# Two product tiles in turn, half a contraction apart, and activations moved by 64 bytes

## The chip, the cores and the metric

The kernel runs on one core of a Trainium2 chip. The metric is device time in microseconds (us) of one execution, lower is better. Engines are named as in the profile: PE is TensorE (matmuls), PEld its weight loads, DVE is VectorE, ACT is ScalarE, POOL is GpSimd, SP issues most DMAs.

## What is computed

A decoder trunk of two residual layers over 256 tokens of width 2048, all in float32. Layer 0 is "even" (an RG-LRU group and an RWKV-7 group behind one input projection), layer 1 is "odd" (an mLSTM block). Each is followed by a gated convolutional FFN. The change works in the odd layer, and by its second part in every product that reads the normed activations:

```
def mlstm_layer(x, norm, w_in, conv_w, conv_b, w_q, w_k, w_v, w_if, b_if, ln_w, skip, w_out):
    h = rms_norm(x, norm)                                  # (256, 2048)
    xm, z = jnp.split(h @ w_in, [C_WIDTH], axis=-1)        # w_in: 2048 x 8192, C_WIDTH 4096
    xc = jax.nn.silu(causal_dwconv(xm, conv_w, conv_b))
    ... # q, k, v, gates, the chunkwise mLSTM per head, layer norm, skip: hs
    return x + (hs * jax.nn.silu(z)) @ w_out               # w_out: 4096 x 2048

def conv_ffn(x, norm, w_gate, w_up, conv_w, conv_b, w_down):
    h = rms_norm(x, norm)
    u = jax.nn.silu(causal_dwconv(h @ w_gate, conv_w, conv_b)) * (h @ w_up)
    return x + u @ w_down
```

## The kernel before

**Tiles.** Everything is held transposed: 128 features on the partitions, 256 tokens along the free dimension. A weight matrix is cut into blocks of 128 x 128, 16 of them to a chunk of 128 x 2048 floats (1024 KB). `chunk` loads one from SP's queue into a `raw` tile (2 buffers) and splits it into a high part `wh` and a low part `wl` of the float32r type, in 4 pieces of 512 columns: ACT rounds (L243), DVE subtracts (L244). `wh` and `wl` have 2 buffers each, so a chunk's parts can be made when the chunk before the last is used up. An activation tile is split likewise: `x[k]`, `ux[k]` and `yx[k]` are tiles of 128 x 2 x 256, and the low part stands ahead of the high part.

**A block step.** One block of weights times one activation tile costs two matmuls in the wide form: `wh` times both parts (512 columns moved, into both halves of a PSUM bank) and `wl` times the high part (256 columns). Each matmul loads its 128 x 128 weights first. The products come in two orders:

- `mm3` (L247 to L261) does one output tile after another; within it each k runs low (L255), then high (L257), only the first k high (L254), then low. `project` (the odd layer's input product `oin`, 64 tiles of 16 blocks, in two stages: 32 tiles `xm`, then 32 tiles `z`) and `flat` (the odd layer's output product `oout`, 16 tiles of 32 blocks, and the even layer's two output products `eoa`, `eob`) use it. The even layer's input product `ein` uses the narrow form of `mm3`: three matmuls of 256 columns (L259 to L261).
- `mm3_pair` (L305 to L313) does two output tiles at once: high, high (L311), low, low (L313), both with the same `x[k]`. The FFN uses it: `fgu` (gate and up, moved operand `x`) and `fd` (down, moved operand `ux`), in tiles named `mp`.

**What sets the order.** The code emits instructions in program order, and the tile framework schedules them onto the engines; each engine then runs its own list in order. Side work is written as generators; `tick` lets each of them emit one more step, once in 4 block steps (`TICK`). In the odd layer's first stage the side work is `head_tile` (per tile: a convolution on ACT and DVE, L406 and L409, and the small products `pv` L932, `pr` L941, `sc` L947); in the second it is `heads_out` (the attention of one head after the other). A finished tile is read out of PSUM by `scaled` (ACT copy L424, DVE add L425, DVE multiply by the norm L427) or by `add_residual` (two DVE adds, L432). The pool `mm_ps` has 3 PSUM banks, tile name `mm`.

**Where the operands lie.** The pools `const`, `raw`, `parts` and `act` are opened in this order and stand behind one another in SBUF; the pools of the layers come behind `act`. `act` holds the residual, `x0` to `x15`, a few work tiles, and, by way of `rstd_steps` and `rsqrt`, the tiles `ms` and `rsq` of 2 floats a partition, each in a slot of 32 bytes. In the built program `wh` and `wl` begin 64 bytes past a multiple of 128, and so do all `x[k]`; `ux`, the odd layer's `yx` and 7 of `eob`'s 8 `yx` begin at a multiple of 128.

Of the kernel before, what the change touches and what calls it, by code (L numbers as in the profile page):

```python
# [17 lines left out]
F32 = mybir.dt.float32  # L18
# [6 lines left out]
P = 128  # L25
T = 256
D = 2048
KD = D // P
# [3 lines left out]
CW = 4096  # L32
# [7 lines left out]
CHEADS = 8  # L40
CTILES = 4
TICK = 4
# [4 lines left out]
SW = [4, 2]  # L47
OWAITS = [5, 2, 4]
AWAITS = [0, 4, 0, 1, 1, 3]


def wait(n):
    for _ in range(n):
        yield
# [52 lines left out]
class Builder:  # L107
    def __init__(self, tc, io, ctx):
        self.tc, self.nc, self.io = tc, tc.nc, io
        self.tile_pool = lambda **k: tc.tile_pool(reuse_waits="tile", **k)  # L110
        nc = self.nc
        self.n = 0
        pool = lambda name, bufs, **k: ctx.enter_context(self.tile_pool(name=name, bufs=bufs, **k))
        self.const = pool("const", 1)
        self.raw = pool("raw", 2)
        self.parts = pool("parts", 2)
        self.act = pool("act", 1)
        self.mm_ps = pool("mm_ps", 3, space=PSUM)
        self.vec_sb = self.const.tile([P, NV], F32, name="vec_sb")
        self.cons = {}  # L120
        self.load_con("con", self.const)
        self.x = [None] * KD
        self.sumsq = None
        self.rstd = None
        self.tasks = []
        self.norm_psum = lambda: self.psum_mm()[:, 0]
# [176 lines left out]
                self.tick()  # L303


    def mm3_pair(self, ps, w, c, x, start, stop):
        TE = self.nc.tensor
        hi = [w[0][:, i:i + P] for i in c]
        lo = [w[1][:, i:i + P] for i in c]
        for i in range(2):  # L310
            TE.matmul(ps[:, i], hi[i], x, start=start, stop=False)  # L311
        for i in range(2):
            TE.matmul(ps[:, i, 1], lo[i], x[:, 1], start=False, stop=stop)  # L313
# [51 lines left out]
    def rstd_steps(self):  # L365
        nc, a = self.nc, self.act
        yield from wait(SW[0])
        ps = self.norm_psum()
        for i in range(2):
            nc.tensor.matmul(ps[:, i:i + 1], self.sumsq[:, i * P:i * P + P], self.con("ones")[:, 0:1],  # L370
                             start=True, stop=True)
        ms = a.tile([P, 2], F32, name=self.name("ms"), tag="ms")
        nc.vector.tensor_scalar(ms, ps[:, 0:2], 1.0 / D, EPS, op0=ALU.mult, op1=ALU.add)
        r = self.rsqrt(a, ms, 2)
        yield from wait(SW[1])
        self.rstd = self.row_bcast(self.norm_psum, a, r, "rstd")

# [482 lines left out]
    def odd(self, gain, folded, fold_pool):  # L860
        nc, tc = self.nc, self.tc
        V, A, TE = nc.vector, nc.scalar, nc.tensor
        io = self.io
        with ExitStack() as es:
            big = es.enter_context(self.tile_pool(name="odd", bufs=1))
            big_tile = lambda dt, n: big.tile([P, CTILES, T], dt, name=self.name(n), tag="big", bufs=17)
            self.load_con("con_odd", big)
            raws, xcs, vs = [], [], []
            gates = big.tile([P, 2, 16], F32, name="gates")
            with ExitStack() as e1:  # L870
                sml = e1.enter_context(self.tile_pool(name="odd1", bufs=2))
                psr = e1.enter_context(self.tile_pool(name="odd1_ps", bufs=2, space=PSUM))
                psa = e1.enter_context(self.tile_pool(name="odd1_acc", bufs=1, space=PSUM))
                wl, wv, fa, fv = folded
                bdm = self.con("bdmask").rearrange("p (g j) -> p g j", j=4)
                four = lambda w: w.unsqueeze(1).to_broadcast([P, 32, 4])
                nc.gpsimd.memset(gates, 0.0)
                ops = (four, bdm, wl, wv, fa, fv)
                self.norm_psum = lambda: psr.tile([P, T], F32, name=self.name("np"), tag="pr")
                ps = self.projections(io["oin"], CHEADS * CTILES)  # L880
                for h in range(CHEADS):
                    xc4, v4 = big_tile(F32, "xc"), big_tile(F32, "v")
                    vt = v4.rearrange("p a b -> p (a b)").rearrange("p (s c) -> p s c", s=2)
                    raw = big.tile([P, 384], F32, name=self.name("raw"), tag="sc", bufs=CHEADS)
                    st = {}
                    for q in range(CTILES):
                        xm = self.scaled(sml, next(ps), 3, "xm", 3)
                        last = self.start(self.head_tile(h, q, xm, xc4[:, q], vt, raw, gates, st, ops, sml, psr, psa))
                    raws.append(raw)
                    xcs.append(xc4)  # L890
                    vs.append(vt)
                self.finish(last)
            fold_pool.close()
            yx = []
            with ExitStack() as e2:
                sml = e2.enter_context(self.tile_pool(name="odd2", bufs=2))
                one = e2.enter_context(self.tile_pool(name="odd2c", bufs=1))
                psw = e2.enter_context(self.tile_pool(name="odd2_ps", bufs=3, space=PSUM))
                pss = e2.enter_context(self.tile_pool(name="odd2_ps2", bufs=2, space=PSUM))
                pw = lambda *s: psw.tile(list(s), F32, name=self.name("pz"), tag="pz")  # L900
                pst = lambda *s: pss.tile(list(s), F32, name=self.name("pt"), tag="pt")
                zs = {}
                nums = self.start(self.heads_out(one, sml, pw, pst, gates, raws, vs, xcs, zs, big_tile, yx))
                for ct in range(CHEADS * CTILES):
                    while len(zs) >= 6:
                        self.tick()
                    z = self.scaled(sml, self.project(io["oin"][32 + ct]), 0, "z", 6)
                    A.activation(z, z, AF.Silu)
                    zs[ct] = z
                self.finish(nums)  # L910
                self.flat(io["oout"], 32, KD, yx, lambda m, ps: self.add_residual(m, ps, gain))

    def head_tile(self, h, q, xm, xc, vt, raw, gates, st, ops, sml, psr, psa):

# [144 lines left out]
    def attend(self, h, sml, pw, pst, raw, v, crow, gm):  # L1059
# [5 lines left out]
        TE.matmul(ps, self.con("ones")[0:8], ch, start=True, stop=True)  # L1065
        yield from wait(AWAITS[0])
        d = sml.tile([P, 384], F32, name=self.name("dec"), tag="dec")
# [4 lines left out]
        V.scalar_tensor_tensor(out=d, in0=raw, scalar=512.0 ** -0.5, in1=d, op0=ALU.mult, op1=ALU.mult)  # L1072
        yield from wait(AWAITS[1])
        ones = self.con("ones")[:, 0:1]
        st = sml.tile([P, 2, 2], F32, name=self.name("st"), tag="st")
        for s in range(2):
# [4 lines left out]
            V.tensor_copy(out=st[:, 0, s:s + 1], in_=ps)  # L1081
        yield from wait(AWAITS[2])
        num = sml.tile([P, CTILES, T], F32, name=self.name("num"), tag="num", bufs=1)
        acc = None
        for q in range(CTILES):
# [8 lines left out]
            else:  # L1094
                V.tensor_tensor(out=sq, in0=acc, in1=sq, op=ALU.add)
                acc = sq
            yield from wait(AWAITS[3])
        yield from wait(AWAITS[4])
        for s in range(2):
# [10 lines left out]
        rs = self.rsqrt(sml, var, 2)  # L1110
        yield from wait(AWAITS[5])
        return self.row_bcast(lambda: pst(P, T), sml, rs, "sbc"), num
# [31 lines left out]
def _by_cols(w):  # L1144

    k, m = w.shape
    return np.ascontiguousarray(w.reshape(k // P, P, m // P, P).transpose(2, 1, 0, 3)).reshape(m // P, P, -1)


def _flat(w):  # L1150

    k, m = w.shape
    t = w.reshape(k // P, P, m // P, P).transpose(2, 0, 1, 3).reshape(-1, 16, P, P)
    return np.ascontiguousarray(t.transpose(0, 2, 1, 3)).reshape(-1, P, 2048)


def _pairs(ws):

    n, k, _, _ = ws.shape
    t = ws.reshape(n, k // P, P, 2, P).transpose(0, 1, 3, 2, 4).reshape(-1, 16, P, P)  # L1160
    return np.ascontiguousarray(t.transpose(0, 2, 1, 3)).reshape(-1, P, 2048)
# [8 lines left out]
def _arrange(I):  # L1170
    I = {k: np.asarray(v) for k, v in I.items()}
    z = lambda *s: np.zeros(s, np.float32)
    o = {"xT": np.ascontiguousarray(I["x"][0].T.reshape(KD, P, T).transpose(1, 0, 2)), **_constants()}
    w = I["even_w_in"][0]
# [4 lines left out]
    m = I["b_mu"][0]  # L1179
# [6 lines left out]
        pieces += [w[:, cols(j)], w[:, AW + j * P:AW + j * P + P]]  # L1186
    o["ein"] = _by_cols(np.concatenate(pieces, 1))
    o["eoa"], o["eob"] = _flat(I["even_w_out"][0][:AW]), _flat(I["even_w_out"][0][AW:])
    o["oin"], o["oout"] = _by_cols(I["odd_w_in"][0]), _flat(I["odd_w_out"][0])
    for l in range(2):  # L1190
        by = lambda n: I[n][l].reshape(D, NF, P).transpose(1, 0, 2)
        o[f"fgu{l}"] = _pairs(np.stack([by("ffn_w_gate"), by("ffn_w_up")], 2))
# [44 lines left out]
```

## Time and profile before

| | |
|---|---|
| median of 3 runs | 2620.32 us (2619.95 to 2620.73) |
| profiled execution, its time / its span | 2621.55 us / 2619.7 us |
| busy in the span | PE 99%, PEld 87%, DVE 71%, ACT 56%, POOL 5% |
| granted TensorE clock | 0.997 of full speed |
| even layer (`ein`, `eoa`, `eob` and side work) | up to 500 us |
| first FFN: `fgu`, `fd` | 500 to 991, 991 to 1234 us |
| odd layer: `xm`, `z`, `oout` | 1234 to 1465, 1465 to 1686, 1687 to 1868 us |
| second FFN: `fgu`, `fd` | 1868 to 2360, 2360 to 2603 us |

The span is the time from the first to the last instruction of the profiled execution. PE's busy share says that it seldom waits for another engine, not that its matmuls follow one another as closely as they could: a record's length holds the pipeline too, and the next matmul starts before it ends. So a product's pace is read here from the starts of its matmuls.

### The profile page before, as it was taken

The numbers are of one execution on the slowest core, as the hardware profiler recorded it, in microseconds if no ns is written. First come the engines' busy times: TensorE is split into PE (matmuls) and PEld (weight loads), VectorE is DVE, ScalarE is ACT, GpSimd is POOL, SyncE is SP. The second block draws the span as 40 slices with busy tenths as digits, with TensorE's granted clock in tenths as the row PEclk, the third lists the DMA queues.
The fourth block names the chain that finished last, engine by engine and source line by source line (L and its number), as shares of the span: only waits on it lengthen the run. The fifth ranks groups of instructions, "written<-read, shape, count | busy, mean of one in ns | idle before, by whom it ended". The sixth has DMA issues, their size and how long they took to land.

```text
span 2619.7 us, 43129 instructions
## 1 busy us (share of the span) xinstructions
PE 2587.5 (99%) x16438; PEld 2272.8 (87%) x16438; DVE 1859.0 (71%) x4205; ACT 1459.0 (56%) x3071; POOL 137.9 (5%) x402
## 2 busy tenths in 40 slices
PE   9999999999999999999999999999999999999997
PEld 8888887888888888888888888888888888888886
DVE  7988888888667665555777787855667666775554
ACT  6766673655555554444666766644455555554443
POOL 1122111000000000000000000000000000000000
PEclk9999999999999999999999999999999999999999
DMA  6434434565555555555444344455555555555553
GB/s 209 154 108 129 134 105 141 185 217 205 185 189 193 193 193 190 189 185 197 149 144 153 134 148 160 144 203 184 181 189 193 193 193 185 187 189 195 184 199 132
DMA packets 67696, 454.41 MB, mean 173 GB/s; under 512 B 9328, under 2 KB 10352, under 8 KB 14240
## 3 DMA queue, kind: packets, MB, share of 16 engines
q1 hardware_dynamic: 62064, 441.69, 48.5%
q0 software_dynamic: 4416, 7.85, 1.1%
q8 instruction: 129, 2.11, 0.3%
q10 hardware_dynamic: 1008, 2.11, 0.2%
q14 instruction: 79, 0.65, 0.1%
HBM read 448.70 MB, written 2.10 MB: 172 GB/s over the span
## 4 chain that ended last, share of the span: by engine, by line
PE 82%; issue 11%; DVE 4%; ACT 1%; POOL 1%; DMA 0%; DVEq 0%; POOLq 0%; ACTq 0%
PE mp L311 31%; PE mp L313 15%; PE mm L257 14%; PE mm L255 8%; PE mm L259 2%; PE mm L260 2%; PE mm L261 2%; PE mm L254 1%; PE sc L947 1%; DVE wl L244 1%; PE pw L669 1%; PE pv L932 1%; PE pz L1087 1%; PE pr L941 1%; POOL rsq L381 0%
## 5 line engine op out<-in xcount | busy, mean ns | idle before, releaser
L244 DVE TENSOR_TENSOR wl<-raw,wh 128x512 fp32r<-128x512 f32 (+1 forms) x1680 | 1091.7, 682 | 511.3 <-ACT wh L243 509.8
L243 ACT CAST wh<-raw 128x512 fp32r<-128x512 f32 (+1 forms) x1680 | 952.7, 617 | 693.4 <-PE mp L311 540.5
L311 PE MATMUL mp<-x,wh 128*128 128x512 f32 x2816 | 884.7, 395 | 0.0
L313 PEld LDWEIGHTS mp<-x,wl 128*128 128x128 f32 x2816 | 529.0, 188 | 125.0
L313 PE MATMUL mp<-x,wl 128*128 128x256 f32 x2816 | 553.1, 278 | 0.0
L311 PE MATMUL mp<-ux,wh 128*128 128x512 f32 x1408 | 437.0, 392 | 0.0
L311 PEld LDWEIGHTS mp<-x,wh 128*128 128x128 f32 x2816 | 428.8, 189 | 0.1
L257 PE MATMUL mm<-x,wh 128*128 128x512 f32 x960 | 341.7, 394 | 0.0
L313 PEld LDWEIGHTS mp<-ux,wl 128*128 128x128 f32 x1408 | 264.4, 188 | 58.3
L255 PE MATMUL mm<-x,wl 128*128 128x256 f32 x1024 | 283.4, 287 | 0.0
L313 PE MATMUL mp<-ux,wl 128*128 128x256 f32 x1408 | 278.0, 279 | 0.0
L257 PE MATMUL mm<-yx,wh 128*128 128x512 f32 x720 | 255.8, 395 | 0.0
L311 PEld LDWEIGHTS mp<-ux,wh 128*128 128x128 f32 x1408 | 213.2, 188 | 0.0
L255 PE MATMUL mm<-yx,wl 128*128 128x256 f32 x768 | 210.6, 284 | 1.7 <-DVE wl L244 1.4
L257 PEld LDWEIGHTS mm<-x,wh 128*128 128x128 f32 x960 | 180.3, 188 | 35.9 <-DVE x L344 0.2
L255 PEld LDWEIGHTS mm<-x,wl 128*128 128x128 f32 x1024 | 193.2, 189 | 7.5 <-DVE yx L202 2.3
L259 PE MATMUL mm<-x,wh 128*128 128x256 f32 x640 | 191.5, 299 | 0.0
L261 PE MATMUL mm<-x,wl 128*128 128x256 f32 x640 | 181.8, 284 | 1.5 <-DVE wl L244 1.5
L260 PE MATMUL mm<-x,wh 128*128 128x256 f32 x640 | 182.1, 284 | 0.0
L257 PEld LDWEIGHTS mm<-yx,wh 128*128 128x128 f32 x720 | 135.2, 188 | 29.6 <-DVE yx L202 0.2
L255 PEld LDWEIGHTS mm<-yx,wl 128*128 128x128 f32 x768 | 143.9, 188 | 7.4 <-DVE wl L244 2.2
L259 PEld LDWEIGHTS mm<-x,wh 128*128 128x128 f32 x640 | 122.5, 191 | 6.5 <-issue 0.9
(360 smaller groups left out, 2628.9 us busy)
## 6 DMA issues: line engine op xcount, KB each, us to landing
raw<-fgu SPq DMA_DIRECT2D x176, 1024.0 KB, 4.9
raw<-fd SPq DMA_DIRECT2D x88, 1024.0 KB, 4.9
raw<-oin SPq DMA_DIRECT2D x64, 1024.0 KB, 4.9
raw<-ein SPq DMA_DIRECT2D x40, 1024.0 KB, 4.9
raw<-oout SPq DMA_DIRECT2D x32, 1024.0 KB, 4.9
raw<-eoa SPq DMA_DIRECT2D x8, 1024.0 KB, 4.9
raw<-eob SPq DMA_DIRECT2D x8, 1024.0 KB, 4.9
wif<-wif POOLq DMA_DIRECT2D x12, 256.0 KB, 4.2
```

What stands on the lines that cost most here:

```text
L243: nc.scalar.copy(hi[:, s], raw[:, s])
L244: nc.vector.tensor_tensor(out=lo[:, s], in0=raw[:, s], in1=hi[:, s].bitcast(F32), op=ALU.subtract)
L254: TE.matmul(ps, hi, x, start=True, stop=False)
L255: TE.matmul(ps[:, 1], lo, x[:, 1], start=False, stop=False)
L257: TE.matmul(ps, hi, x, start=False, stop=stop)
L259: TE.matmul(ps, hi, x[:, 0], start=start, stop=False)
L260: TE.matmul(ps, hi, x[:, 1], start=False, stop=False)
L261: TE.matmul(ps, lo, x[:, 1], start=False, stop=stop)
L311: TE.matmul(ps[:, i], hi[i], x, start=start, stop=False)
L313: TE.matmul(ps[:, i, 1], lo[i], x[:, 1], start=False, stop=stop)
L669: TE.matmul(ps[H[h], c], lt[H[h], c], x[H[h], c], start=True, stop=True)
L932: TE.matmul(ps[:, s], xm[:, 3 + s * P:3 + s * P + P], bv, start=True, stop=True)
```

## The change

**Order.** The three products of the odd layer no longer use `mm3`. `turns` yields steps: in the middle of a product a step holds two block steps, one of the second half of tile s-1's contraction and one of the first half of tile s's. `staggered` emits a step as high, high, low, low (L333 of the new kernel), each high-low pair with its own `x[k]`. Half a tile at the start and half a tile at the end of each product run alone. One tile still ends after every 16 block steps (32 in `oout`). The weights are laid out on the host in the order in which they are used, so that a chunk still holds 16 blocks in a row.

**Place.** `ms` and `rsq` of the norms move to a pool of their own, `short`, that is opened between `parts` and `act`. Its 64 bytes move all of `act` by 64 bytes; what stands behind `act` stays where it was.

| begins at, modulo 128 | before | after |
|---|---|---|
| `wh`, `wl` | 64 | 64 |
| `x0` to `x15` (also `yx` of `eoa`) | 64 | 0 |
| `ux`, `yx` of `oout` and `eob` | 0 (one `yx` of `eob`: 64) | 0 |

```
+def turns(n, nk):
+    h = nk // 2
+    for s in range(n + 1):
+        a = [(s - 1, k) for k in range(h, nk)] if s else []
+        b = [(s, k) for k in range(h)] if s < n else []
+        yield from zip(a, b) if a and b else ((t,) for t in a + b)
...
         self.parts = pool("parts", 2)
+        self.short = pool("short", 1)
         self.act = pool("act", 1)
...
+    def staggered(self, src, n, nk, x):
+        TE = self.nc.tensor
+        ps, w, at = {}, None, 0
+        for step in turns(n, nk):
+            ops = []
+            for m, k in step:
+                if at % 16 == 0:
+                    w = self.chunk(src[at // 16])
+                c = slice(at % 16 * P, at % 16 * P + P)
+                at += 1
+                if k == 0:
+                    ps[m] = self.psum_mm()
+                ops.append(((ps[m], w[0][:, c], x[k], k == 0, False),
+                            (ps[m][:, 1], w[1][:, c], x[k][:, 1], False, k == nk - 1)))
+            for group in zip(*ops):
+                for out, lhsT, rhs, start, stop in group:
+                    TE.matmul(out, lhsT, rhs, start=start, stop=stop)
+            if at % TICK == 0:
+                self.tick()
+            for m, k in step:
+                if k == nk - 1:
+                    yield ps.pop(m)
...
-        ms = a.tile([P, 2], F32, name=self.name("ms"), tag="ms")
+        ms = self.short.tile([P, 2], F32, name=self.name("ms"), tag="ms")
...
-        r = self.rsqrt(a, ms, 2)
+        r = self.rsqrt(self.short, ms, 2)
...
-                ps = self.projections(io["oin"], CHEADS * CTILES)
+                ps = self.staggered(io["oxm"], CHEADS * CTILES, KD, self.x)
+                ps = chain([next(ps), next(ps)], ps)
...
+                ps = self.staggered(io["oz"], CHEADS * CTILES, KD, self.x)
...
-                    z = self.scaled(sml, self.project(io["oin"][32 + ct]), 0, "z", 6)
+                    z = self.scaled(sml, next(ps), 0, "z", 6)
...
-                self.flat(io["oout"], 32, KD, yx, lambda m, ps: self.add_residual(m, ps, gain))
+                for m, ps in enumerate(self.staggered(io["oout"], KD, 32, yx)):
+                    self.add_residual(m, ps, gain)
```

PE's list before, in the middle of the `xm` stage, where one tile ends and the next begins (a name is followed by its buffer numbers; `mm_1838` and `mm_1850` are two tiles in a row, `wh_1836` and `wh_1848` two chunks):

```order
L255 MATMUL mm_1838_14381<-x_1709_13609,wl_1837_14372 128x256
L257 MATMUL mm_1838_14381<-x_1709_13609,wh_1836_14371 128x512
L947 MATMUL sc_1806_14208<-r_1820_14255,xc_1758_13910 128x272
L947 MATMUL sc_1807_14209<-r_1820_14255,xc_1758_13910 128x144
L941 MATMUL pr_1845_14443<-xc_1810_14220,bl_1829_14323 128x256
L254 MATMUL mm_1850_14463<-x_1558_11795,wh_1848_14453 128x512
L255 MATMUL mm_1850_14463<-x_1558_11795,wl_1849_14454 128x256
L255 MATMUL mm_1850_14463<-x_1560_11802,wl_1849_14454 128x256
L257 MATMUL mm_1850_14463<-x_1560_11802,wh_1848_14453 128x512
```

And now, at the corresponding place (`mm_1828` ends, `mm_1839` goes on with its second half, `mm_1851` begins):

```order
L333 MATMUL mm_1828_14328<-x_1709_13612,wl_1848_14440 128x256
L333 MATMUL mm_1839_14401<-x_1623_12576,wl_1848_14440 128x256
L986 MATMUL sc_1810_14240<-r_1821_14275,xc_1762_13942 128x272
L986 MATMUL sc_1811_14241<-r_1821_14275,xc_1762_13942 128x144
L980 MATMUL pr_1849_14475<-xc_1814_14252,bl_1830_14343 128x256
L333 MATMUL mm_1839_14401<-x_1644_12833,wh_1847_14439 128x512
L333 MATMUL mm_1851_14483<-x_1558_11798,wh_1847_14439 128x512
L333 MATMUL mm_1839_14401<-x_1644_12833,wl_1848_14440 128x256
L333 MATMUL mm_1851_14483<-x_1558_11798,wl_1848_14440 128x256
```

The two matmuls of a block step no longer stand together; the chunk, which changed with the tile, is now in its middle there and changes half a tile later. The small products stand where they stood.

DVE's list before, around the read-out of one `xm` tile (`wl` is the low part of the weights, `ccv` the convolution, `bl` and `bv` small weights of the head):

```order
L425 TENSOR_TENSOR xm_1859_14521<-mm_1850_14463,xm_1859_14521 128x256
L427 TENSOR_TENSOR xm_1859_14521<-xm_1859_14521,bc_1728_13734 128x256
L923 TENSOR_TENSOR bl_1868_14556<-wl_6715,con_odd_sb_13622 128x128
L244 TENSOR_TENSOR wl_1876_14605<-raw_1874_14602,wh_1875_14604 128x512 x2
L409 SCALAR_TENSOR_TENSOR ccv_1867_14550<-xm_1859_14521,vec_sb_70,ccv_1867_14550 128x256
L244 TENSOR_TENSOR wl_1876_14605<-raw_1874_14602,wh_1875_14604 128x512
L409 SCALAR_TENSOR_TENSOR ccv_1867_14550<-xm_1859_14521,vec_sb_70,ccv_1867_14550 128x256
L244 TENSOR_TENSOR wl_1876_14605<-raw_1874_14602,wh_1875_14604 128x512
L409 SCALAR_TENSOR_TENSOR ccv_1867_14550<-xm_1859_14521,vec_sb_70,ccv_1867_14550 128x256
L938 TENSOR_TENSOR hv_1844_14415<-pv_1871_14571,hv_1844_14415 128x34
```

And now:

```order
L460 TENSOR_TENSOR xm_1863_14553<-mm_1839_14401,xm_1863_14553 128x256
L462 TENSOR_TENSOR xm_1863_14553<-xm_1863_14553,bc_1726_13735 128x256
L962 TENSOR_TENSOR bl_1869_14576<-wl_6718,con_odd_sb_13625 128x128
L444 SCALAR_TENSOR_TENSOR ccv_1868_14570<-xm_1863_14553,vec_sb_73,ccv_1868_14570 128x256 x3
L255 TENSOR_TENSOR wl_1886_14672<-raw_1884_14669,wh_1885_14671 128x512
L964 TENSOR_TENSOR bv_1881_14651<-wqkv_6717,con_odd_sb_13625 128x128
L977 TENSOR_TENSOR hv_1845_14435<-pv_1872_14591,hv_1845_14435 128x34
L255 TENSOR_TENSOR wl_1886_14672<-raw_1884_14669,wh_1885_14671 128x512 x3
L460 TENSOR_TENSOR xm_1877_14629<-mm_1851_14483,xm_1877_14629 128x256
```

The three convolution steps now run in a row, and all four pieces of the weights' low part come behind them, right ahead of the next tile's read-out. On ACT the order has moved likewise: the last rounding pieces of `wh` (now L254) stand right ahead of the next tile's PSUM copy (now L459), where before they stood right behind it.

More of the change, by code (lines that the diff above doesn't have):

```diff
@@ L1154, in _flat, with _staggered @@
     return np.ascontiguousarray(t.transpose(0, 2, 1, 3)).reshape(-1, P, 2048)
+def _staggered(w):
+    k, m = w.shape
+    t = w.reshape(k // P, P, m // P, P).transpose(2, 0, 1, 3)
+    i = np.array([x for step in turns(m // P, k // P) for x in step])
+    t = t[i[:, 0], i[:, 1]].reshape(-1, 16, P, P)
+    return np.ascontiguousarray(t.transpose(0, 2, 1, 3)).reshape(-1, P, 2048)
 def _pairs(ws):
@@ L1188, in _arrange @@
     o["eoa"], o["eob"] = _flat(I["even_w_out"][0][:AW]), _flat(I["even_w_out"][0][AW:])
-    o["oin"], o["oout"] = _by_cols(I["odd_w_in"][0]), _flat(I["odd_w_out"][0])
+    o["oxm"], o["oz"] = _staggered(I["odd_w_in"][0][:, :CW]), _staggered(I["odd_w_in"][0][:, CW:])
+    o["oout"] = _staggered(I["odd_w_out"][0])
     for l in range(2):
```

## Prediction

> **What bounds the kernel now.** I read the page's busy shares and the clock first.
>
> ```profile
> PE 2587.5 (99%) x16438; PEld 2272.8 (87%) x16438; DVE 1859.0 (71%) x4205; ACT 1459.0 (56%) x3071; POOL 137.9 (5%) x402
> PEclk9999999999999999999999999999999999999999
> ```
>
> PE is never idle for long and the clock is granted in full. So time can only come from the pace of PE's matmuls, or be lost by new waits of PE. Next, what PE waits for, in the view of the waits on PE: the two longest, and the one on weights in the `mm` tiles.
>
> ```profile
> PE pw L835 <- DVE lru_x L409: 8.3, 7, 1.8
> PE mm L370 <- DVE ssq L359: 2.7, 1, 2.7
> ...
> PE mm L255 <- DVE wl L244: 1.4, 1, 1.4
> ```
>
> The long ones lie in the even layer. In the products that the change reorders there is next to no wait to remove, so all of its gain must be pace. The pace is the start-to-start time of matmuls: the count of the tiles' matmuls in windows that lie well inside one product, the two FFN products first, `oout` last (columns: window, its length, PE's busy time and count).
>
> ```profile
> 520.00:960.00 440.00, 440.00 (x2528) 383.87 (x2527) 33.03 (x79) 29.22 (x80) 1.00 0.56 195
> 1000.00:1220.00 220.00, 220.00 (x1277) 193.63 (x1277) 11.15 (x28) 0.00 (x0) 1.00 0.57 195
> ...
> 1700.00:1860.00 160.00, 160.00 (x913) 139.84 (x913) 12.71 (x30) 0.00 (x0) 1.00 0.54 191
> ```
>
> A window counts about two matmuls that only reach into it, so I take 2526, 1275 and 911: 174.19 ns each in `fgu`, 172.55 in `fd`, 175.63 in `oout`. A block step is two matmuls: 348.4, 345.1 and 351.3 ns. `fgu` and `fd` run the same code in the same order (high, high, low, low) with the same PSUM tiles; what differs is the moved operand, which begins at 64 modulo 128 in `fgu`, as the weights do, and at 0 in `fd`. The timeline shows where the few ns lie; first `fgu`, then `fd` (start, length, line; x2 is two matmuls in a row):
>
> ```profile
> 700.29 0.62 PE L311 MATMUL mp<-x,wh 128*128 128x512 f32 x2
> 700.75 0.40 PE L313 MATMUL mp<-x,wl 128*128 128x256 f32 x2
> 700.99 0.63 PE L311 MATMUL mp<-x,wh 128*128 128x512 f32 x2
> 701.46 0.39 PE L313 MATMUL mp<-x,wl 128*128 128x256 f32 x2
> 701.68 0.62 PE L311 MATMUL mp<-x,wh 128*128 128x512 f32 x2
> ...
> 1099.87 0.62 PE L311 MATMUL mp<-ux,wh 128*128 128x512 f32 x2
> 1100.33 0.39 PE L313 MATMUL mp<-ux,wl 128*128 128x256 f32 x2
> 1100.56 0.62 PE L311 MATMUL mp<-ux,wh 128*128 128x512 f32 x2
> 1101.01 0.40 PE L313 MATMUL mp<-ux,wl 128*128 128x256 f32 x2
> 1101.25 0.62 PE L311 MATMUL mp<-ux,wh 128*128 128x512 f32 x2
> ```
>
> Two high matmuls take 0.46 to 0.47 us in `fgu` and 0.45 to 0.46 in `fd`, two low ones 0.22 to 0.24 in both. A whole round of four is 0.70 (700.29 to 700.99) against 0.69 (1099.87 to 1100.56). The pattern repeats round after round, so chance meetings with DVE or ACT are not its cause.
>
> The first stages of the odd layer have small products between, so I take clean stretches of low-high pairs, by the starts of the low matmuls:
>
> ```profile
> 1441.61 0.28 PE L255 MATMUL mm<-x,wl 128*128 128x256 f32 x1
> ...
> 1443.34 0.28 PE L255 MATMUL mm<-x,wl 128*128 128x256 f32 x1
> ...
> 1444.53 0.28 PE L255 MATMUL mm<-x,wl 128*128 128x256 f32 x1
> ...
> 1446.64 0.28 PE L255 MATMUL mm<-x,wl 128*128 128x256 f32 x1
> ```
>
> The first stretch holds 5 block steps in 1.73 us (346 ns each), the second 6 in 2.11 (352). Mixed: about 350.
>
> **The change, part by part.** The sum goes against the profiled execution, 2621.55 us: a span of 2619.7 and 1.85 around it. That is 1.2 above the median of 2620.32.
>
> *Order in the odd layer.* No matmul, DMA, read-out or split is added or removed, and SP loads the same 96 chunks in the order of their use; 1024 block steps of `oin` and 512 of `oout` run high, high, low, low. A row of exactly this order with the moved operand at 0 and the weights at 64 is `fd`: 345.1 ns. `oin`: (349.9 - 345.1) x 1024 = 4.9 us. `oout`: (351.3 - 345.1) x 512 = 3.2 us. `fd`'s two high matmuls share one activation tile, the staggered ones don't; no row prices that, and since both tiles lie a multiple of 2048 bytes apart I cost it at nothing. From below the gain is bounded by `fgu`'s rate in the same order: 1.5 x 1024 + 2.9 x 512 = 3.0 us. Half a tile runs alone at both ends of each product, 8 + 8 + 8 + 8 + 16 + 16 = 64 block steps at the old pace, which takes back 0.3. Small products that stood behind a high matmul now stand behind a low one; they are as many as before, and I cost this at nothing.
>
> *Place of `x`.* The FFN's code is untouched, but `fgu` now has `fd`'s places. Its matmuls are counted by these rows of the page:
>
> ```profile
> L311 PE MATMUL mp<-x,wh 128*128 128x512 f32 x2816 | 884.7, 395 | 0.0
> ...
> L313 PE MATMUL mp<-x,wl 128*128 128x256 f32 x2816 | 553.1, 278 | 0.0
> ```
>
> 5632 x (174.19 - 172.55) = 9.2 us. `fd` itself is not moved: nothing. `ein` is moved too; it has 1920 matmuls of 256 columns (640 blocks by three, L259 to L261), and they follow one another so:
>
> ```profile
> 300.35 0.28 PE L260 MATMUL mm<-x,wh 128*128 128x256 f32 x1
> 300.47 0.28 PE L261 MATMUL mm<-x,wl 128*128 128x256 f32 x1
> 300.59 0.28 PE L259 MATMUL mm<-x,wh 128*128 128x256 f32 x1
> 300.71 0.28 PE L260 MATMUL mm<-x,wh 128*128 128x256 f32 x1
> 300.83 0.28 PE L261 MATMUL mm<-x,wl 128*128 128x256 f32 x1
> ```
>
> That is 0.12 us each. No row has this order with `x` at 0; a pair of low matmuls takes 0.23 in `fd` (1100.33 to 1100.56) and 0.24 in `fgu` (700.75 to 700.99), 115 to 120 ns each. I take no change, and 2.5 ns on either side as bounds: 4.8 us up or down. `eoa` has 256 block steps at the pace of `oout` or `oin`, 1.4 ns apart: at most 0.4 us, left out.
>
> All of this rests on the place being what divides `fgu` from `fd`. The Trainium skill has a rule against it: "TensorE: Matmul & The Clock Gate" (Part 2, step 1) says that TensorE reads moved operand and weights through two independent SBUF ports, and that loading the next weights takes no bandwidth from the running matmul. By that rule the place could not matter and the second term would be 0; the 174.19 against 172.55 of the trace doesn't agree, unless something else divides the two products.
>
> *Read-out and weights.* A tile's PSUM bank is wanted again when the next tile but two begins, now one tile after its end (about 7 us in `xm`) where it was two. The read-out is one copy and one add, 0.37 and 0.42 us by the rows below: covered. In `xm` the weights' low parts now stand in DVE's list behind the whole convolution and right ahead of the next read-out. What DVE and ACT do there, and what they wait for (the window is 28 tiles; the last columns are busy time, mean ns, idle time before):
>
> ```profile
> L244 DVE TENSOR_TENSOR wl<-raw,wh 128x512 fp32r<-128x512 f32 x112 | 74.6, 680 | 0.0
> L243 ACT CAST wh<-raw 128x512 fp32r<-128x512 f32 x112 | 64.1, 625 | 0.0
> L409 DVE SCALAR_TENSOR_TENSOR ccv<-xm,vec_sb,ccv 128x256 f32<-128x256 f32 x84 | 39.8, 474 | 0.0
> ...
> L406 ACT ACTIVATE ccv<-xm,vec_sb 128x256 f32<-128x256 f32 x28 | 17.3, 617 | 0.0
> ...
> L427 DVE TENSOR_TENSOR xm<-xm,bc 128x256 f32<-128x256 f32 x28 | 12.2, 436 | 0.9
> L425 DVE TENSOR_TENSOR xm<-mm,xm 128x256 f32<-128x256 f32 x28 | 11.9, 424 | 51.9 <-ACT xm L424 51.9
> L920 ACT ACTIVATE xc<-ccv 128x256 f32<-128x256 f32 x28 | 11.7, 418 | 8.0 <-DVE ccv L409 7.9
> ...
> L424 ACT COPY xm<-mm 128x256 f32<-128x256 f32 x27 | 10.1, 372 | 47.6 <-PE mm L257 47.6
> ...
> L923 DVE TENSOR_TENSOR bl<-wl,con_odd_sb 128x128 f32<-128x128 f32 x29 | 8.1, 280 | 0.0
> L925 DVE TENSOR_TENSOR bv<-wqkv,con_odd_sb 128x128 f32<-128x128 f32 x28 | 7.7, 276 | 0.0
> ```
>
> DVE waits 51.9 / 28 = 1.85 us a tile for the next tile's end: that is its slack. The new order makes it wait for ACT's first step of the convolution with only `bl` between (617 - 280 = 337 ns), and, behind the convolution, for `xc` and the first `wh` with only `bv` between (418 + 625 - 276 = 767 ns): 1.1 us. A tile gets shorter by 16 x 4.8 ns = 0.08. Left: 0.67 us a tile. So DVE keeps up, and PE, which finds its weights made half a tile ahead, waits for nothing. Cost: 0.
>
> Sum: -4.9 - 3.2 + 0.3 - 9.2 = -17.0, so 2604.5 for the profiled execution and, 1.2 below, **2603.3** for the median.
>
> **The rivals.**
> *Place counts for nothing* (the skill's rule), something else made `fd` fast: only the order acts, at `fgu`'s rate, 3.0 - 0.3 = 2.7 us: 2617.6. For it: `oout` has its operands at 0 and 64 already and is no faster than `oin`. Against it: the two FFN products differ in little else.
> *Staggering brings nothing* (two activation tiles in turn break what makes the paired order close, and the odd layer keeps its 350 ns), while the place works: 2620.3 - 9.2 = 2611.1. That the reordered part doesn't do what it says is this case.
> *Place harms*: `fgu` stays, `ein` loses 4.8, the odd layer gains 2.7: 2622.4, no change that can be told.
> *DVE and ACT set the pace in `xm`*, the side on which it gets slower. Once DVE is late, its loop no longer waits for PE: 424 + 436 + 617 + 3 x 474 + 418 + 625 + 4 x 680 = 6662 ns, and some more where a head ends, against 230.6 / 32 = 7.2 us that a tile takes on PE now:
>
> ```profile
> 1234.40:1465.00 230.60, 230.51 (x1342) 203.53 (x1341) 172.23 (x437) 145.22 (x336) 17.56 (x93) 1.00 0.43 150
> ```
>
> A loop of up to 7.2 costs nothing, since the weights are half a tile (3 us) early and 31 tiles of 0.1 use that up. It decides when it takes what the rest gains: (17.0 + 3) / 31 = 0.65 us a tile over PE's 7.1, so from 7.75 us. At 8.1 us 31 x 1.0 - 3 = 28 are lost: 2631.
>
> **How the numbers follow.** A measurement of this kernel can tell about 0.2% (5.2 us) from no change. My case, both parts at `fd`'s pace: 0.60, from 2598.5 to 2608 by `ein`'s bounds. Place counts for nothing: 0.17, of which 0.03 ends under 2615.1 because the order alone may reach more of `fd`'s rate. Staggering brings nothing: 0.08. Place harms: 0.06. DVE's loop: 0.09, of which 0.04 is slower by over 0.2%; 0.03 takes only part of the gain; 0.02 ends level. Faster: 0.60 + 0.03 + 0.08 + 0.03 = 0.74. Slower: 0.04 and 0.01 from a harmful place: 0.05. The same: 0.21. The range goes from 2597 to 2618, which takes in the first three cases but for their edges.
>
> **What would show it.** Right: `fgu`'s count in a window of 440 us rises from 2528 to about 2552; the odd layer's stages shrink by about 2.5, 2.5 and 3; PE's view of waits gains no row in the odd layer; `fd` stays at 1277 in 220 us. Wrong: `fgu` stays at 2528 (place), `oout` stays at 913 in 160 us (order), PE waits for `wl` or for a read-out in `xm`, or `ein`'s step of 0.12 moves.

## The result, and the profile after

The changed kernel takes 2606.02 us (median of 4 runs, 2604.45 to 2609.24), the kernel before 2620.52 (4 runs, 2619.95 to 2620.73): a ratio of 0.9945, with a 95% interval of 0.9934 to 0.9957. That is 14.5 us less, where 17.0 were predicted. Unless a profile below is said to be of another kernel, it is the profiled execution of the changed kernel: 2604.45 us, a span of 2602.6. Three executions in the experiments ran at a granted clock of 0.516, 0.654 or 0.775 and are left out of every ratio; all profiles read below ran at 0.997 or 0.998.

PE is as busy as before, at the full clock (the page):

```profile
PE 2567.6 (99%) x16438; PEld 2264.4 (87%) x16438; DVE 1869.0 (72%) x4205; ACT 1470.6 (57%) x3071; POOL 142.5 (5%) x402
PEclk9999999999999999999999999999999999999999
```

The windows that carried the prediction, for the tiles `mp` (`fgu`, then `fd`) and `mm` (`oout`, ten us earlier than before because the stage is):

```profile
520.00:960.00 440.00, 440.00 (x2553) 387.37 (x2552) 33.45 (x80) 29.19 (x79) 1.00 0.57 198
1000.00:1220.00 220.00, 220.00 (x1278) 193.58 (x1277) 11.16 (x28) 0.00 (x0) 1.00 0.55 192
...
1690.00:1850.00 160.00, 160.00 (x929) 140.80 (x929) 11.89 (x28) 0.00 (x0) 1.00 0.55 192
```

`fgu` goes from 2528 matmuls in 440 us to 2553, `oout` from 913 in 160 us to 929, and `fd` stays. Twice as many `fgu` matmuls as `fd` ones now fit into twice the time: the two products have one pace.

A window that begins with the first matmul of a product and ends with the start of its last gives the length of the stage; its count says that it holds the whole. First `oin` (2048 matmuls) and `ein` (1920) before, then after:

```profile
1234.41:1685.59 451.18, 389.76 (x2048) 314.93 (x2048) 26.62 (x63) 23.30 (x63) 1.00 0.43 149
...
26.82:379.27 352.45, 258.95 (x1920) 238.08 (x1920) 16.10 (x39) 0.00 (x0) 1.00 0.40 130
```

```profile
1225.61:1675.75 450.14, 387.93 (x2048) 321.69 (x2048) 26.48 (x63) 23.33 (x63) 1.00 0.43 149
...
26.47:375.15 348.68, 254.01 (x1920) 233.14 (x1920) 16.14 (x39) 0.00 (x0) 1.00 0.40 132
```

All stages in this way (from first start to last start, us):

| stage | before | after | difference | predicted |
|---|---|---|---|---|
| `ein` | 352.45 | 348.68 | -3.8 | 0 (bounds +-4.8) |
| `eoa`, `eob` | 118.47 | 118.39 | -0.1 | at most 0.4, left out |
| `fgu`, both layers | 2 x 491.24 | 486.57 + 486.60 | -9.3 | -9.2 |
| `fd`, both layers | 242.80 + 242.81 | 2 x 242.77 | -0.1 | 0 |
| `oin` | 451.18 | 450.14 | -1.0 | -4.9, and +0.15 for half tiles |
| `oout` | 181.17 | 178.80 | -2.4 | -3.2, and +0.15 for half tiles |

The sum is -16.6 and the spans differ by 17.1, the medians by 14.5. The profiled execution of before is 1.0 above its median and that of after 1.6 below. Part of that is the clock. This window of the kernel before (5 us within `ein`; the third number from the end is the granted clock) holds a stretch at half clock; in the changed kernel's profile the stretch from 40 to 160 us has none:

```profile
105.00:110.00 5.00, 5.00 (x26) 4.56 (x26) 4.00 (x12) 3.18 (x8) 2.19 (x4) 0.66 0.37 126
```

```profile
40.00:160.00 120.00, 114.03 (x1011) 105.87 (x1010) 104.78 (x280) 85.91 (x180) 20.55 (x47) 1.00 0.42 140
```

It is worth at most 0.34 x 5 = 1.7 us, all of it in `ein`. This stage also differs from one execution to the next: over the profiles of this case and of the experiments below it took 349.9 to 352.4 us in the four in which `x` lies as far from the weights (modulo 128) as before, and 348.7 to 349.4 in the six in which it lies as after. The two means are 2.0 us apart, so the 3.8 of this pair is more than the change is worth.

`ein`'s step of 0.12 us moved, which the prediction had named among the signs that it is wrong (ten steps between the first row and the last):

```profile
300.74 0.28 PE L271 MATMUL mm<-x,wh 128*128 128x256 f32 x1
300.86 0.28 PE L272 MATMUL mm<-x,wl 128*128 128x256 f32 x1
...
301.76 0.28 PE L271 MATMUL mm<-x,wh 128*128 128x256 f32 x1
301.88 0.28 PE L272 MATMUL mm<-x,wl 128*128 128x256 f32 x1
```

1.14 us for ten steps is 0.114 each here; over all undisturbed neighbours between 150 and 370 us (674 before, 681 after) the mean of high-to-low and low-to-high steps went from 119.6 to 117.3 ns.

PE's waits in the odd layer (1225 to 1856 us), where before this view was empty:

```profile
PE pt L432 <- DVE dg L431: 0.7, 1, 0.7
PE pv L971 <- DVE hv L975: 0.4, 1, 0.4
PE pv L971 <- DVE hv L977: 0.2, 1, 0.2
```

None is for weights or for a read-out of `mm`. The first comes 6 us into `oout`, where the scale of the last head's norm is spread over the partitions (`dg`); the last comes at the end of `xm`. The second comes early in `xm`, at 1251 us: `hv` reads `pv` out of PSUM, and in DVE's list it stood behind two pieces of `wl`:

```profile
1250.12 1.28 DVE L255 TENSOR_TENSOR wl<-raw,wh 128x512 fp32r<-128x512 f32 x2
...
1251.32 0.18 DVE L975 COPY hv<-pv 128x34 f32<-128x34 f32 x1
...
1251.65 0.73 PE L971 MATMUL pv<-bv,xm 128*128 128x145 f32 x4 [0.42 <-DVE hv L975]
```

The profile of the order alone (below) has the same three waits, 0.7, 0.3 and 0.2 us, and that of the place alone none, so they come with the order. In the read-out of `mm` itself DVE and ACT came near to holding PE up. In 28 tiles of `xm` (1240 to 1440 us; the last columns are busy time, mean ns, idle time before and its releaser):

```profile
L460 DVE TENSOR_TENSOR xm<-mm,xm 128x256 f32<-128x256 f32 x28 | 11.8, 422 | 0.6 <-ACT xm L459 0.5
```

```profile
L459 ACT COPY xm<-mm 128x256 f32<-128x256 f32 x28 | 10.5, 373 | 13.5 <-PE mm L333 13.3
```

DVE no longer waits for the read-out (51.9 us before); its idle time now lies between it and ACT. ACT still waits for PE's tile, 13.3 / 28 = 0.48 us each: that is what is left of the slack, where the prediction had worked out 0.67.

### The profile page after: what moved, and what is told of

Same layout as the page of the kernel before. It is cut to its first block, busy times and chain, and to the rows that moved or that the text cites. A ratio compares the mean times of both kernels' runs of the same rounds, so it can differ in the third digit from the quotient of the medians.

```text
span 2602.6 us, 43142 instructions
## 1 busy us (share of the span) xinstructions
PE 2567.6 (99%) x16438; PEld 2264.4 (87%) x16438; DVE 1869.0 (72%) x4205; ACT 1470.6 (57%) x3071; POOL 142.5 (5%) x402
## 4 chain that ended last, share of the span: by engine, by line
PE 79%; issue 11%; DVE 6%; ACT 2%; DMA 1%; POOL 1%; ACTq 0%; DVEq 0%; POOLq 0%
PE mp L346 30%; PE mm L333 20%; PE mp L348 15%; PE mm L270 2%; PE mm L271 1%; PE mm L272 1%; PE mm L268 1%; DVE wl L255 1%; PE mm L266 1%; PE sc L986 1%; PE pv L971 1%; PE pz L1126 1%; DMA blocks<-dc 1%; PE pr L980 0%; POOL rsq L416 0%
## 5 line engine op out<-in xcount | busy, mean ns | idle before, releaser
L254 ACT CAST wh<-raw 128x512 fp32r<-128x512 f32 (+1 forms) x1680 | 955.5, 617 | 696.2 <-PE mp L346 530.2
L346 PE MATMUL mp<-x,wh 128*128 128x512 f32 x2816 | 874.1, 392 | 0.0
L333 PE MATMUL mm<-x,wh 128*128 128x512 f32 x1024 | 333.8, 406 | 0.0
L333 PEld LDWEIGHTS mm<-x,wl 128*128 128x128 f32 x1024 | 192.2, 188 | 42.8 <-issue 0.2
L333 PE MATMUL mm<-x,wl 128*128 128x256 f32 x1024 | 205.8, 280 | 0.0
L270 PE MATMUL mm<-x,wh 128*128 128x256 f32 x640 | 188.8, 295 | 0.0
L272 PE MATMUL mm<-x,wl 128*128 128x256 f32 x640 | 179.2, 280 | 1.8 <-DVE wl L255 1.8
L271 PE MATMUL mm<-x,wh 128*128 128x256 f32 x640 | 179.5, 281 | 0.0
L333 PEld LDWEIGHTS mm<-x,wh 128*128 128x128 f32 x1024 | 158.9, 188 | 5.3 <-ACT z L459 2.7
L333 PE MATMUL mm<-yx,wh 128*128 128x512 f32 x512 | 160.4, 392 | 0.0
L270 PEld LDWEIGHTS mm<-x,wh 128*128 128x128 f32 x640 | 120.1, 188 | 6.5 <-issue 0.9
L272 PEld LDWEIGHTS mm<-x,wl 128*128 128x128 f32 x640 | 120.0, 187 | 2.4 <-DVE wl L255 2.2
L271 PEld LDWEIGHTS mm<-x,wh 128*128 128x128 f32 x640 | 120.3, 188 | 0.7
L333 PEld LDWEIGHTS mm<-yx,wl 128*128 128x128 f32 x512 | 96.2, 188 | 19.9
```

The costliest lines, as they stand in the source:

```text
L254: nc.scalar.copy(hi[:, s], raw[:, s])
L270: TE.matmul(ps, hi, x[:, 0], start=start, stop=False)
L271: TE.matmul(ps, hi, x[:, 1], start=False, stop=False)
L272: TE.matmul(ps, lo, x[:, 1], start=False, stop=stop)
L333: TE.matmul(out, lhsT, rhs, start=start, stop=stop)
```

## The experiments

**The two parts apart.** The kernel before with only the pool `short`:

```
+        self.short = pool("short", 1)
         self.act = pool("act", 1)
...
-        ms = a.tile([P, 2], F32, name=self.name("ms"), tag="ms")
+        ms = self.short.tile([P, 2], F32, name=self.name("ms"), tag="ms")
...
-        r = self.rsqrt(a, ms, 2)
+        r = self.rsqrt(self.short, ms, 2)
```

> The place alone: the kernel before with ms and rsq in a pool ahead of act, so x begins at 0 modulo 128 and the weights at 64; every product in its old order. Theory (the moved operand's place beside the weights' sets the pace): fgu runs at fd's 172.55 ns a matmul, about 2552 in its window of 440 us and 9.2 us less; ein's step falls from 0.120 to 0.118 us as in the changed kernel, 4 us less; the odd layer's oin, now at oout's places in oout's order, goes from 349 to oout's 351 ns a block step, 2 us more. Sum: 2609, between 2606.5 and 2611. Rival (the place counts for nothing, the gain in fgu and ein came from somewhere else in the change): all stages as before, 2620.5.

And the changed kernel with these lines undone:

```
-        self.short = pool("short", 1)
...
-        ms = self.short.tile([P, 2], F32, name=self.name("ms"), tag="ms")
+        ms = a.tile([P, 2], F32, name=self.name("ms"), tag="ms")
...
-        r = self.rsqrt(self.short, ms, 2)
+        r = self.rsqrt(a, ms, 2)
```

> The order alone: the changed kernel with ms and rsq left in act, so x begins at 64 like the weights. Theory (place): fgu stays at 2528 in 440 us and ein at 0.120 us a step; in the odd layer oout, whose operands lie as in the changed kernel, gains its 2.4 us; oin runs at fgu's old 348.4 ns in clean stretches, 0.7 us less than before, and the small products' breaks take that back. Sum: 2618, between 2617 and 2619.5. Rival (the order brings all): 2606.

Measured: the place alone 2610.6 us (ratio 0.9964, 0.9951 to 0.9978), the order alone 2617.8 (0.9990, 0.9980 to 1.0000, which takes in no change, so the stages have to tell). Windows of the place alone: `fgu`, `oout`, and the whole of `oin` and `ein`:

```profile
520.00:960.00 440.00, 440.00 (x2553) 387.35 (x2552) 33.58 (x80) 29.47 (x80) 1.00 0.58 197
...
1700.00:1860.00 160.00, 160.00 (x914) 139.81 (x914) 11.89 (x28) 0.00 (x0) 1.00 0.56 192
...
1226.77:1679.24 452.47, 391.02 (x2048) 315.62 (x2048) 26.69 (x63) 23.41 (x63) 1.00 0.44 149
26.77:376.27 349.50, 255.90 (x1920) 235.13 (x1920) 16.14 (x39) 0.00 (x0) 1.00 0.40 132
```

The same of the order alone:

```profile
520.00:960.00 440.00, 440.00 (x2528) 383.90 (x2527) 33.50 (x80) 29.45 (x80) 1.00 0.57 195
...
1700.00:1860.00 160.00, 160.00 (x929) 140.93 (x928) 12.58 (x30) 0.00 (x0) 1.00 0.57 195
...
1233.08:1684.56 451.48, 389.27 (x2047) 321.96 (x2048) 26.55 (x63) 23.28 (x63) 1.00 0.44 149
26.61:377.98 351.37, 259.44 (x1920) 238.58 (x1920) 16.15 (x39) 0.00 (x0) 1.00 0.40 130
```

The last window of the place alone begins 0.46 us ahead of `ein`'s first matmul, so that stage took 349.0 us. `fgu` and `ein` follow the place and nothing else (`ein`'s step, read as above, is 117.3 ns with the place alone and 119.7 with the order alone), `oout` the order and nothing else. `oin` needs both: the place alone makes it 1.3 us longer (the old low-high order likes `x` at 64 better), the order alone 0.3 longer, both together 1.0 shorter. So here the place and the order are no two gains that add up. The prediction did price the pair from a row that has both, `fd`; what that row doesn't have is the small products in between.

**Is it the place, or the distance to the weights?** The changed kernel with the weights' parts moved as well:

```
-        self.parts = pool("parts", 2)
-
         self.short = pool("short", 1)
+        self.parts = pool("parts", 2)
         self.act = pool("act", 1)
```

> The changed kernel with the small pool opened ahead of the weights' parts, so the weights too move by 64 bytes: wh, wl, x, ux and yx all begin at 0 modulo 128. Theory A (what counts is the distance of moved operand and weights): every product now has the distance that fgu had before; fgu goes back to 2528 in 440 us (+9.2 us), fd falls from 1277 to about 1265 in 220 us (+4.7 us over both), ein back to 0.120 (+4), oout and oin lose 1 to 3 together: 2624 to 2628, slower than before. Theory B (what counts is where the moved operand begins by itself, 0 being better): as the changed kernel, 2606.

2624.05 us, slower than before (1.0016, 1.0006 to 1.0025). `fgu`, `fd` and `oout`:

```profile
520.00:960.00 440.00, 440.00 (x2528) 383.93 (x2528) 33.51 (x80) 29.54 (x80) 1.00 0.57 195
1000.00:1220.00 220.00, 220.00 (x1265) 191.94 (x1265) 11.17 (x28) 0.00 (x0) 1.00 0.57 192
...
1700.00:1860.00 160.00, 160.00 (x920) 139.58 (x920) 11.89 (x28) 0.00 (x0) 1.00 0.56 189
```

`fd`, which no part of the change touches, loses its pace (1277 to 1265) because its weights moved: theory A. The mirror image says the same from the other side, with the weights at 0 and all activations at 64:

```
-        self.parts = pool("parts", 2)
-
         self.short = pool("short", 1)
+        self.parts = pool("parts", 2)
+        self.gap = pool("gap", 1)
+        self.gap.tile([P, 16], F32, name="pad", tag="pad")
         self.act = pool("act", 1)
```

> The operands changed over: the weights' parts begin at 0 modulo 128 and x, ux and all yx at 64, where the changed kernel has 64 and 0. Theory A (only the distance counts): every pace as in the changed kernel, fgu 486.6 us, fd 242.8, ein's step 0.1175, oout 178.8, 2606. Theory B (it is the weights at 64 with the moved operand at 0 that is good, by their own places): fgu 491.2 or more, fd 245 or more, 2624 or more.

2605.7 us (0.9943, 0.9920 to 0.9965), every pace as in the changed kernel:

```profile
520.00:960.00 440.00, 440.00 (x2552) 387.39 (x2552) 33.34 (x80) 29.43 (x80) 1.00 0.58 198
1000.00:1220.00 220.00, 220.00 (x1277) 193.60 (x1277) 11.17 (x28) 0.00 (x0) 1.00 0.57 191
```

**Which distances?** A padding in the pool `short` of 16 floats moves `act` by another 64 bytes:

```
         self.short = pool("short", 1)
+        self.short.tile([P, 16], F32, name="pad", tag="pad")
```

> The changed kernel with 64 bytes of padding behind ms and rsq, so that x, ux and yx all begin 128 bytes further off the weights' parts than in the kernel before for x: at 64 modulo 128 like the parts, but not modulo 256. Theory A (the distance counts modulo 128): as with all operands at 0, fgu 491.25 us, fd 245.1, ein's step 0.120, oin about 451.8, oout about 180.4, 2624. Theory B (only a distance of 0 modulo 256 or more is bad): fgu 486.6, fd 242.8, ein 0.1175, total 2606.

One execution took 2623.8 us, which is theory A. For a profile that can be read for a pace, once more:

> The kernel with all moved operands another 128 bytes off once more, for a profile at the full clock, since its first one ran at a granted clock of 0.654. Theory A (modulo 128): fgu 491.25 us, fd 245.1, oout 180.4, total 2624. Theory B (modulo 256 or more): fgu 486.6, fd 242.8, total 2606.

2625.5 us, `fgu` and `fd`:

```profile
520.00:960.00 440.00, 440.00 (x2528) 385.17 (x2527) 33.38 (x80) 29.57 (x80) 1.00 0.58 195
1000.00:1220.00 220.00, 220.00 (x1265) 192.59 (x1264) 11.14 (x28) 0.00 (x0) 1.00 0.57 192
```

The counts are those of distance 0: for `fgu` and `fd` what counts repeats with 128 bytes. `ein` follows less well: its step is 118.6 ns here, where all operands at 0 gave 119.5. Now a quarter of that, by leaving `rsq` in `act` (`x` 32 past the weights):

```
-        r = self.rsqrt(self.short, ms, 2)
+        r = self.rsqrt(a, ms, 2)
```

> The changed kernel with rsq left in act, so that act moves by 32 bytes and x begins at 96 modulo 128, 32 off the weights; ux and the odd yx stay at 0, 64 off. Theory A (any distance but a whole line is good): fgu 486.6 us, ein's step 0.1175, 2606. Theory B (the half line itself is what is good): fgu 491.2 and ein 0.120 as before, oin as with the order alone, 451.5: 2618. Theory C (the gain grows with the distance): fgu half way, 488.9, ein 0.1187, 2612. fd 242.8 and oout 178.8 in all three.

2611.4 us (0.9968, 0.9954 to 0.9981), with `fgu` half way, as theory C had it, but `ein`'s step at 117.4 ns, as theory A had it:

```profile
520.00:960.00 440.00, 440.00 (x2541) 388.03 (x2540) 33.51 (x80) 29.57 (x80) 1.00 0.58 195
```

And three quarters, with a padding of 8 floats:

```
         self.short = pool("short", 1)
+        self.short.tile([P, 8], F32, name="pad", tag="pad")
```

> The changed kernel with 32 bytes of padding behind ms and rsq, so that x, ux and yx all begin at 32 modulo 128, 96 past the weights' parts (or 32 ahead of them). Theory A (any distance but a whole line is good): fgu 486.6 us, fd 242.8, ein's step 0.1175, oin 450.1, oout 178.8, 2606. Theory B (the half line itself is what is good): as with all operands at 0, fgu 491.25, fd 245.1, oout 180.4, 2624. Theory C (graded): half way, 2615.

2648.1 us (1.0106, 1.0076 to 1.0135): slower than all three theories and than the kernel before.

```profile
520.00:960.00 440.00, 440.00 (x2493) 382.70 (x2492) 32.56 (x78) 28.81 (x78) 1.00 0.57 193
1000.00:1220.00 220.00, 220.00 (x1248) 191.37 (x1247) 11.20 (x28) 0.00 (x0) 1.00 0.55 188
```

In that run `x` itself begins off a multiple of 64, so the same distance with the weights there instead:

```
+        self.gap = pool("gap", 1)
+        self.gap.tile([P, 8], F32, name="gap", tag="gap")
         self.parts = pool("parts", 2)
         self.short = pool("short", 1)
+        self.short.tile([P, 8], F32, name="pad", tag="pad")
```

> The changed kernel with 32 bytes ahead of the weights' parts and 32 bytes behind ms and rsq: wh and wl begin at 96 modulo 128, x, ux and yx at 64, so the moved operand lies 96 past the weights, as in the run with x at 32, but now it is the weights that begin off a multiple of 64. Theory A (only the distance counts): fgu 498.2 us, fd 248.6, total 2648. Theory B (the loss of that run came from the moved operand beginning off a multiple of 64): fgu 491 or less, 2625 or less.

2648.4 us (1.0106, 1.0088 to 1.0125), `fgu` x2493 again. At 0, at 64 and at 96 two sets of places with the same distance give the same count: it is the distance, and not the places, that sets the pace of this order.

```profile
520.00:960.00 440.00, 440.00 (x2493) 383.78 (x2492) 32.52 (x78) 28.95 (x78) 1.00 0.57 192
```

**Why `oin` gained so little.** In the changed kernel's `xm`, small products break into the paired order twice a tile (`sc` and `pr`, then `pv`). The starts of the two highs of each round, and of the last small product ahead of them:

```profile
1340.48 0.59 PE L980 MATMUL pr<-xc,bl 128*128 128x256 f32 x2
1340.72 0.82 PE L333 MATMUL mm<-x,wh 128*128 128x512 f32 x2
...
1341.62 0.63 PE L333 MATMUL mm<-x,wh 128*128 128x512 f32 x2
...
1342.32 0.62 PE L333 MATMUL mm<-x,wh 128*128 128x512 f32 x2
...
1343.01 0.62 PE L333 MATMUL mm<-x,wh 128*128 128x512 f32 x2
...
1343.70 0.66 PE L971 MATMUL pv<-bv,xm 128*128 128x145 f32 x4
1344.10 0.71 PE L333 MATMUL mm<-x,wh 128*128 128x512 f32 x2
...
1344.89 0.62 PE L333 MATMUL mm<-x,wh 128*128 128x512 f32 x2
```

The round behind the first break takes 0.90 us, the next 0.70, then 0.69; behind `pv` it is 0.79. With one break a tile instead:

```
-OWAITS = [5, 2, 4]
+OWAITS = [3, 4, 4]
```

> The changed kernel with the small product pv given out at the same turn of the side work as the other small products of its tile (the three waits of the odd layer's side work 3, 4, 4 where they were 5, 2, 4), so that a tile of xm is broken into once where it was twice. Theory (each break costs the paired order some 0.01 to 0.02 us because the first rounds behind it are longer, 696 where 690 ns follow): xm gets 0.3 to 0.6 us shorter, 234.1 to about 233.6, the rest stays: 2605.5. Rival (the breaks cost nothing beyond their own matmuls): xm stays at 234.1. Either way the total can hardly tell, so the stage is read from the trace.

2605.4 us (0.9945, 0.9927 to 0.9963). `pv` now follows `pr` at once, and the round behind the one break takes 0.79 us, where those behind the two took 0.90 and 0.79:

```profile
1341.42 0.72 PE L333 MATMUL mm<-x,wh 128*128 128x512 f32 x2
...
1342.21 0.62 PE L333 MATMUL mm<-x,wh 128*128 128x512 f32 x2
...
1342.90 0.62 PE L333 MATMUL mm<-x,wh 128*128 128x512 f32 x2
```

The expectation's 234.1 for `xm` counted to the first small product of `z`. From the first of `xm`'s 1024 matmuls to the first of `z`, the changed kernel, then this one with its `z`:

```profile
1225.61:1455.20 229.59, 195.83 (x1024) 162.24 (x1025) 13.48 (x32) 11.93 (x32) 1.00 0.43 150
```

```profile
1226.26:1454.63 228.37, 185.51 (x1024) 158.16 (x1025) 13.56 (x32) 11.91 (x32) 1.00 0.44 151
1454.63:1675.41 220.78, 192.77 (x1024) 159.47 (x1024) 13.04 (x31) 11.36 (x31) 1.00 0.44 148
```

1.2 us less, with 33 breaks for 60: the direction that the theory had, at two to four times its size. About half is a quicker pace between the breaks (345.6 ns a block step for 347.0, over all undisturbed neighbours in `xm`), the other half the breaks themselves. The same idea in `z`, where `pz` now comes out two by two (beside the one break a tile in `xm`):

```
-            yield from wait(AWAITS[3])
+            yield from wait(2 * AWAITS[3] if q % 2 else 0)
```

> The kernel with one break a tile in xm, and beside it the products pz of the attention in z given out two by two instead of one by one, 16 breaks fewer in z. Theory (a break costs the paired order more than its own matmuls; 27 breaks fewer in xm gave 1.21 us, 45 ns each): z from 220.8 to about 220.0 us, all else as with one break a tile, 2604.7. Rival (xm gained for another reason, such as where pv stands): z stays at 220.8.

2603.8 us (0.9938, 0.9923 to 0.9953), and `z`, with 43 breaks for 58, 0.65 us shorter:

```profile
1454.67:1674.80 220.13, 188.42 (x1024) 158.43 (x1024) 12.98 (x31) 11.37 (x31) 1.00 0.44 149
```

43 ns for each break that is gone, as in `xm` (45). Whether the kernel before would gain as much from fewer breaks was not run. Last, the staggered order for `eoa` and `eob` on top of this:

```
-            self.flat(self.io["eoa"], 8, KD, yx[:8], lambda m, ps: self.add_residual(m, ps, False))
+            for m, ps in enumerate(self.staggered(self.io["eoa"], KD, 8, yx[:8])):
+                self.add_residual(m, ps, False)
...
-            self.flat(self.io["eob"], 8, KD, yx[8:], lambda m, ps: self.add_residual(m, ps, gain))
+            for m, ps in enumerate(self.staggered(self.io["eob"], KD, 8, yx[8:])):
+                self.add_residual(m, ps, gain)
...
-    o["eoa"], o["eob"] = _flat(I["even_w_out"][0][:AW]), _flat(I["even_w_out"][0][AW:])
+    o["eoa"], o["eob"] = _staggered(I["even_w_out"][0][:AW]), _staggered(I["even_w_out"][0][AW:])
```

> The former, and the even layer's eoa and eob in the staggered order too (256 block steps). Theory: clean stretches there gain 2 to 4 ns a block step, but some 100 breaks by other products take that back: 118.4 us to between 117.4 and 118.6. Rival (the order alone is worth its full 4 ns everywhere): 117.3 us or less. Total 2604 to 2605, about 1 to 2 us below the changed kernel's 2606.

2602.6 us (0.9933, 0.9920 to 0.9945), with `eoa` and `eob` (512 matmuls) at 117.39 us:

```profile
378.36:495.75 117.39, 96.99 (x512) 78.97 (x512) 25.47 (x62) 0.00 (x0) 1.00 0.45 149
```

That is 1.0 less and at the edge between the theory and its rival, so it doesn't tell them apart: the breaks there took back less than I thought. By the stages this version is 1.6 + 1.0 (`oin` and the even outputs) under the changed kernel. The intervals of the two ratios overlap, so the totals alone don't show it.

## Why the prediction was right, and where it was not

**`fgu`: right.** The term was -9.2, measured -9.3, and the count of about 2552 came out at 2553. Its reason was that only the place of the moved operand divides `fgu` from `fd`; the place alone gives the same count, the order alone 2528. So the rivals in which the place counts for nothing, or harms, are out. The Trainium skill's rule in "TensorE: Matmul & The Clock Gate" (Part 2, step 1), two independent read ports, would leave no room for the place; that doesn't agree with 2528 and 2553 in two kernels that differ in the place alone. What the prediction called the place is the distance from the weights.

**`ein`: the value taken was wrong, the bounds held.** I took no change between ends of 4.8 us; the step went from 119.6 to 117.3 ns, near the 2.5 of the lower end, and the stage lost 3.8 us in this pair of profiles and 2.0 on the mean of all. The step that failed is the choice of the middle between two ends of equal standing. Nothing in the profile before told the sign, since the distance does not do the same to every order: `ein`'s gains, `oin`'s old one loses.

**`oout`: nearly right.** -3.2 and half of the 0.3 for half tiles were predicted, -2.4 measured. Over all undisturbed neighbours the pace went from 350.7 to 345.4 ns, 2.7 us, where I had 351.3 and `fd`'s 345.1. That two activation tiles alternate costs at most 0.3 ns a block step, and the rival in which staggering brings nothing is out. PE's wait for the last head's norm takes about 0.6 us back; two slow steps fewer give 0.3.

**`oin`: the term that failed, "(349.9 - 345.1) x 1024 = 4.9 us".** Measured -1.0, less than the 1.5 x 1024 that I had put as its bound from below. I counted over all neighbouring `mm` matmuls but those at breaks: 906 block steps before at 349.3 ns, 907 after at 347.1. So the pace of before was 0.6 lower than the 349.9 of the term (0.5 us), which the two stretches shown there don't give either (11 steps in 3.84 us, 349.1); the 117 steps at breaks don't have this pace to gain (0.6); between breaks the paired order doesn't reach `fd`'s 345.1 (2.0 x 907 = 1.8 us); and the breaks and the steps right behind them cost 0.9 us more. Together, before rounding, 3.9. The failed sentence is the one on the small products: "they are as many as before, and I cost this at nothing". The runs with fewer breaks show that each is worth about 44 ns in this order, part of it in the pace between them. About half of the 0.9 is a single tile: at 1251 us the interval from the matmul ahead of `pv` to the one behind it, less that matmul's own 230 or 115 ns, is 1057 ns, with PE's wait for `hv` in it, and the longest of before was 576. In the other 28 tiles it rose from 397 to 401 ns. What the rest is, is open.

**Read-out and weights: right for the products' own tiles, not for `pv`.** PE has no wait for weights or for a read-out of `mm` in the odd layer, and 0.48 us a tile of slack where 0.67 were left by the working. The rival in which DVE and ACT set the pace was that near. But I had written that PE's view of waits gains no row in the odd layer, and it gained three, 1.3 us together. One of them is for `pv`'s read-out `hv`, which my working of DVE's list had left out.

`ein` gained some 2 to 4 us more than I took and `oin` 3.9 less. It is luck that the two misses have opposite signs, so that the sum came out closer than its terms.

## What to carry to other kernels

Where two products run the same code at paces that differ by a per cent, compare where their operands begin: the distance of the moved operand from the weights, modulo 128 bytes, moved `fgu`'s time from 1.0% less to 1.4% more than at distance 0, and a few bytes of padding set it. A gain in pace that is read from a stretch without foreign matmuls holds only for the steps that run so, and each break has a price of its own (44 ns here), so fewer and longer breaks were better. Two changes in the same place can need each other, as order and place did in `oin`; even a row that has both, as `fd` was, prices them only if it has the same foreign matmuls in between.

## What the hardware showed that was not expected

The pace of `fgu` (order high, high, low, low) against the distance of the moved operand from the weights, modulo 128 bytes:

| distance | `fgu`, us | a block step, ns | in 440 us | runs |
|---|---|---|---|---|
| 0 | 491.24 | 348.9 | 2528 | before; all at 0; 128 further |
| 32 | 489.0 | 347.3 | 2541 | `x` at 96, weights at 64 |
| 64 | 486.57 | 345.6 | 2553 | after; mirror image |
| 96 | 498.2 | 353.8 | 2493 | two, with other places of each |

32 to one side gains half of what 64 does (1.6 ns of 3.3); 32 to the other side, which is 96, loses 4.9. DVE and ACT have the same work in all of these. `ein`'s step (256 columns, one tile) follows another curve: 119.5 to 119.7 ns at 0 and at 96, 117.3 at 64, and 117.4 at 32 already. What in the reading of the operands makes it so was not shown, nor whether other types or sizes have it; and the old order of `oin` (low, high, one tile) goes the other way, 1.3 us longer at 64 than at 0.
